# Strassen-type products for the feed-forward up projections of a two-layer hybrid decoder trunk

## The chip, the cores and the metric

The kernel runs on one NeuronCore of one Trainium2 chip. The metric is the device time of one execution in microseconds (us), the median of several runs. Engines are named as the profile names them: PE is TensorE's matmul, PEld its weight load, DVE is VectorE, ACT is ScalarE, POOL is GpSimd, SP is SyncE, whose queue issues the DMAs.

## The reference

Two layers on x of 1024 tokens x 1024 channels in float32. Layer 0 mixes tokens with forgetting attention, layer 1 with a Conformer convolution module; each mixer is followed by a gated feed-forward block with a causal convolution of width 3.

```python
for i in range(2):
    h = rms_norm(x, mixer_gain)
    x = x + (fox_attention if i == 0 else conformer_conv)(h, ...)
    h = rms_norm(x, ffn_gain)
    x = x + conv_ffn(h, w_up, w_dw, b_dw, w_down)

def conv_ffn(h, w_up, w_dw, b_dw, w_down):      # w_up (1024, 5632), w_down (2816, 1024)
    u = causal_dwconv(h @ w_up, w_dw) + b_dw    # width 3
    gate, val = split(u, 2)
    return (silu(gate) * val) @ w_down

def conformer_conv(h, ...):                     # inner width 1024
    a, g = split(h @ w_pw1 + b_pw1, 2)
    u = causal_dwconv(a * sigmoid(g), w_dw) + b_dw   # width 31
    return silu(rms_norm(u, ln_g)) @ w_pw2 + b_pw2
```

## The kernel before, in words

All matrix products run in a split form: each float32 operand is written as a high part (rounded to the matmul's type by an ACT cast) and a low part (the remainder, a subtraction on POOL or DVE), and `mm3` makes three matmuls of them: high x high, high x low, low x high. A weight tile comes by `weight`: DMA into `raw`, then `split` into `whi` (ACT, L132) and `wlo` (POOL, L133). The matmuls themselves all stand on L138 to L140, so they are told apart by the tile that they write: `up` and `pw` (`pw1`) for the projections up, `dn` for the projections down, `wops` for the attention's output projection, `pj` for its inputs, `nps` for the transposes in a norm.

The order of instructions on each engine is made when the kernel is built: a scheduler takes the work in the order in which the program text emits it (earlier is more urgent) and places an instruction when its inputs and its buffer are there. Emission order is set by Python generators that are stepped against each other.

Tokens are held as two halves of 512. The normed, transposed activations of a half are `hthi` and `htlo`, 8 tiles of 128 channels by 512 tokens. For a feed-forward half, `ffn` runs over 22 channel steps `f`. `up_tile(f)` makes the gate tile and the value tile, each 8 x 3 = 24 matmuls of 128x128 weights on 512 tokens into one PSUM bank; ACT scales the bank into `acc` (L214), DVE adds the two earlier taps (L219), for the second half also the taps that reach into the first half's last tokens (`edge`, L224), ACT applies Silu to the gate (L228), DVE multiplies (L233) and the product is split into `ahi`, `alo` (L236, L237), which stay in SBUF. Every four steps, `down_half` multiplies these by the matching rows of w_down into one of two `dn` banks, 12 matmuls for a block of 128 tokens by 512 channels, and DVE adds the bank to x (L193; L176 in `down`).

x stays in SBUF as 8 tiles of 128 tokens. After the last addition to a block of tokens, `norm_block` norms and transposes it: ACT squares and sums (L110), POOL makes the reciprocal root (L102, L103), DVE scales (L112), PE transposes (L119), ACT and DVE write the high and low parts (L123, L127).

The convolution module of a half is `conv`: `glu` makes two banks of `pw1` (48 matmuls) and `u`; `taps_of` sums 31 taps, 21 of them on DVE (L718, into PSUM) and 10 on ACT and POOL (L722, L723); after all eight channel tiles come the norm (`sqa`, L732) and the projection `pw2`, whose bias POOL adds to x beforehand (L668). While a half is in `conv`, its x is parked in DRAM (`xd`).

The two layers' feed-forward and convolution work is laid side by side by the emission order: layer 0 half 0's feed-forward first, then layer 0 half 1's together with the convolution of half 0 (2 feed-forward steps to 3 convolution steps), then layer 1 half 0's feed-forward together with the convolution of half 1, then layer 1 half 1's. At each change, the first items of the next are alternated with the last of the one before.

Of the kernel before, what the change touches and what calls it, by code (L numbers as in the profile page):

```python
# [43 lines left out]
RAW_BUFS = 2  # L44
WHI_BUFS = 5
WLO_BUFS = 5
ACC_BUFS = 4
ACT_BUFS = 6
# [4 lines left out]
FFN_ITEMS = 88  # L53
LEAD = 4
LAG = 6
TAIL = 2
RATIO = (2, 3)
GAP = 3


class Trunk:
    def __init__(self, ctx, tc):
# [4 lines left out]
        self.hp = ctx.enter_context(tc.tile_pool(name="ht", bufs=1, reuse_waits="tile"))  # L67
# [22 lines left out]

    def ht_half(self, h):
        return tuple(
            self.hp.tile([P, KT, 512], F32R, tag=f"{m}{h}", name=self.n(f"{m}{h}")) for m in ("hthi", "htlo")
        )
# [10 lines left out]
    def norm_block(self, scr, psum, tag, xt, gain, ht, tb, stag="scr"):  # L105
# [7 lines left out]
        hi, lo = ht[tb // 4]  # L113
        c = slice((tb % 4) * P, (tb % 4 + 1) * P)
        for q in range(KT // 4):
            ps = psum.tile([P, 4, P], F32, tag=tag, name=self.n("nps"))
            for j in range(4):
                k = 4 * q + j
                nc.tensor.transpose(ps[:, j, :], hn[:, k * P : (k + 1) * P], self.ident)  # L119
            for j in range(4):  # L120
                k = 4 * q + j
                g = gain[:, k : k + 1]
                nc.scalar.activation(hi[:, k, c], ps[:, j, :], AF.Copy, scale=g)  # L123
            for j in range(4):
                k = 4 * q + j
                g = gain[:, k : k + 1]
                nc.vector.scalar_tensor_tensor(  # L127
                    lo[:, k, c], ps[:, j, :], g, f32(hi[:, k, c]), op0=ALU.mult, op1=ALU.subtract
                )

# [4 lines left out]
    def mm3(self, out, lh, ll, rh, rl, start, stop):  # L135

        nc = self.nc
        nc.tensor.matmul(out, lh, rh, start=start, stop=False)  # L138
        nc.tensor.matmul(out, lh, rl, start=False, stop=False)  # L139
        nc.tensor.matmul(out, ll, rh, start=False, stop=stop)  # L140
# [14 lines left out]
    def weight(self, src, shape):  # L155

        raw = self.wp.tile(shape, F32, tag="raw", name=self.n("raw"), bufs=RAW_BUFS)
        self.nc.sync.dma_start(raw, src)
        hi = self.wp.tile(shape, F32R, tag="whi", name=self.n("whi"), bufs=WHI_BUFS)
        lo = self.wp.tile(shape, F32R, tag="wlo", name=self.n("wlo"), bufs=WLO_BUFS)  # L160
        self.split(hi, lo, raw)
        return hi, lo

    def down(self, xs, h, lhs, rows, after):

        nc = self.nc
        ws = [self.weight(r, [P, D]) for r in rows]
        for b in range(4):
            tb = 4 * h + b
            c = slice(b * P, (b + 1) * P)  # L170
            for nh in range(2):
                m = slice(nh * 512, (nh + 1) * 512)
                ps = self.pdn.tile([P, 512], F32, tag="dn", name=self.n("dn"))
                for j, (hi, lo) in enumerate(lhs):
                    self.mm3(ps, hi[:, c], lo[:, c], ws[j][0][:, m], ws[j][1][:, m], j == 0, j == len(lhs) - 1)
                nc.vector.tensor_tensor(xs[tb][:, m], xs[tb][:, m], ps, op=ALU.add)  # L176
            if after is not None:
                after(tb)
            yield

    def down_half(self, xs, h, lhs, rows, nh):
# [3 lines left out]
        ws = [self.weight(r[:, m].rearrange("(k p) n -> p k n", p=P), [P, 2, 512]) for r in rows]  # L185
        for b in range(4):
            tb = 4 * h + b
            c = slice(b * P, (b + 1) * P)
            ps = self.pdn.tile([P, 512], F32, tag="dn", name=self.n("dn"))
            for j, (hi, lo) in enumerate(lhs):  # L190
                wh, wl = (w[:, j % 2, :] for w in ws[j // 2])
                self.mm3(ps, hi[:, c], lo[:, c], wh, wl, j == 0, j == len(lhs) - 1)
# [3 lines left out]
    def ffn(self, l, xs, h, ht, w_up, w_down, tab, edge, after):  # L196
# [7 lines left out]
        def up_tile(f):  # L204
            accs = []
            for s in range(2):
# [23 lines left out]
                if s == 0:  # L230
                    yield
# [695 lines left out]
```

## Time and profile before

| what | value |
|---|---|
| median of 3 runs | 2415.11 us (2413.39 to 2418.46) |
| profiled execution, its own time | 2417.31 us |
| span of that execution, first to last instruction | 2415.6 us |
| PE, PEld busy | 98%, 84% |
| DVE, ACT, POOL busy | 60%, 50%, 53% |
| mean granted PE clock | 0.994 |
| DMA | 235.40 MB, mean 97 GB/s |
| attention and its output projection end | about 667 us into the span |

Busy time of PE is a matmul's modelled duration, and neighbours overlap, so 98% does not say by itself that PE could not go faster. Idle time that is listed in front of a group of instructions is put down to what ended it. Times in the views below are us from the start of the span unless they end in ns.

### The profile page before, as it was taken

To read this page: it belongs to the slowest core of one execution; us is meant where nothing else is said; L and a number is where in the kernel's file an instruction comes from. 1 tells how busy PE (TensorE), PEld (TensorE's weight loads), DVE (VectorE), ACT (ScalarE), POOL (GpSimd) and SP (SyncE) were. 2 spreads that over 40 slices of the span, in tenths; PEclk is the share of its full clock that TensorE was granted. 3 is DMA by queue.
4 is the path that set the end of the run, shared out by engine and by line. 5 is a ranking of instruction groups with operands and counts; after the bars stand their busy time and mean duration, and the time that the engine had idled before them with its cause. 6 is when DMAs were issued, how large, how long until landed. Compare 5 with 4: busy or idle time off the path is not lost.

```text
span 2415.6 us, 32653 instructions
## 1 busy us (share of the span) xinstructions
PE 2361.5 (98%) x11822; PEld 2028.0 (84%) x11822; DVE 1457.3 (60%) x2773; ACT 1200.6 (50%) x2241; POOL 1274.4 (53%) x886
## 2 busy tenths in 40 slices
PE   7899999989999999999999999999999999999999
PEld 6899999988888888888878878788888887888887
DVE  5577777776353333376868775747767656644444
ACT  6466666665253333355555552545655543333332
POOL 2355544543054444466777763648778644444442
PEclk9999999999999999999999999999999999999999
DMA  4222222154033333243233333333233233333332
GB/s 127 64 79 80 80 76 76 58 178 141 5 118 96 96 97 96 88 133 94 88 104 88 97 109 118 114 96 105 88 99 102 88 130 114 105 105 96 96 96 79
DMA packets 308978, 235.40 MB, mean 97 GB/s; under 512 B 12328, under 2 KB 272208, under 8 KB 308816
## 3 DMA queue, kind: packets, MB, share of 16 engines
q1 hardware_dynamic: 308816, 233.32, 31.6%
q8 instruction: 93, 1.52, 0.3%
q14 instruction: 69, 0.57, 0.1%
HBM read 209.61 MB, written 15.27 MB: 93 GB/s over the span
## 4 chain that ended last, share of the span: by engine, by line
PE 81%; DVE 9%; ACT 3%; POOL 2%; issue 2%; DMA 2%; SPq 0%; POOLq 0%; ACTq 0%; DVEq 0%
PE up L139 11%; PE up L140 11%; PE up L138 11%; PE dn L138 6%; PE dn L140 6%; PE dn L139 6%; PE pj L138 4%; PE pj L139 4%; PE pj L140 4%; PE pT L482 2%; DVE cacc L718 2%; PE s L453 2%; PE pw L139 1%; PE pw L138 1%; DVE acc L219 1%
## 5 line engine op out<-in xcount | busy, mean ns | idle before, releaser
L133 POOL TENSOR_TENSOR wlo<-raw,whi 128x1024 fp32r<-128x1024 f32 (+1 forms) x340 | 804.1, 2372 | 650.7 <-ACT whi L132 633.5
L139 PE MATMUL up<-htlo,whi 128*128 128x512 f32 x1408 | 548.9, 390 | 0.0
L140 PE MATMUL up<-hthi,wlo 128*128 128x512 f32 x1408 | 548.5, 390 | 0.0
L138 PE MATMUL up<-hthi,whi 128*128 128x512 f32 x1408 | 548.0, 390 | 0.0
L132 ACT CAST whi<-raw 128x1024 fp32r<-128x1024 f32 (+2 forms) x344 | 353.8, 1030 | 376.7 <-PE dn L140 157.8
L219 DVE SCALAR_TENSOR_TENSOR acc<-up,ffntab,acc 128x511 f32<-128x511 f32 x352 | 262.3, 745 | 351.0 <-ACT edge L217 200.0
L138 PEld LDWEIGHTS up<-hthi,whi 128*128 128x128 f32 x1408 | 264.3, 188 | 54.7
L139 PEld LDWEIGHTS up<-htlo,whi 128*128 128x128 f32 x1408 | 264.4, 188 | 54.5
L140 PEld LDWEIGHTS up<-hthi,wlo 128*128 128x128 f32 x1408 | 264.4, 188 | 54.2
L138 PE MATMUL dn<-whi,ahi 128*128 128x512 f32 x704 | 277.0, 393 | 7.6 <-DVE x L193 7.6
L140 PE MATMUL dn<-whi,alo 128*128 128x512 f32 x704 | 275.4, 391 | 1.0 <-DVE alo L237 1.0
L139 PE MATMUL dn<-wlo,ahi 128*128 128x512 f32 x704 | 275.3, 391 | 0.0
L718 DVE SCALAR_TENSOR_TENSOR cacc<-u,ctaps,cacc 128x512 f32<-128x512 f32 x320 | 240.8, 753 | 7.4
L193 DVE TENSOR_TENSOR x<-x,dn 128x512 f32<-128x512 f32 x176 | 119.8, 681 | 167.7 <-PE dn L140 167.6
L723 POOL TENSOR_TENSOR pacc<-pacc,prod 128x512 f32<-128x512 f32 x144 | 194.3, 1349 | 33.3 <-ACT prod L722 27.7
L138 PE MATMUL pj<-whi,hthi 128*128 128x384 f32 (+1 forms) x512 | 180.9, 354 | 6.3 <-ACT sqr L380 3.5
L139 PE MATMUL pj<-wlo,hthi 128*128 128x384 f32 (+1 forms) x512 | 178.8, 349 | 0.5 <-DVE wlo L133 0.5
L140 PE MATMUL pj<-whi,htlo 128*128 128x384 f32 (+1 forms) x512 | 179.1, 350 | 0.0
L102 POOL TENSOR_SCALAR ss<-ss 128x4 f32<-128x4 f32 (+1 forms) x96 | 20.7, 215 | 275.9 <-ACT hn L110 124.5
L138 PEld LDWEIGHTS dn<-whi,ahi 128*128 128x128 f32 x704 | 133.0, 189 | 37.7 <-DVE x L193 9.8
L236 ACT CAST ahi<-acc 128x512 fp32r<-128x512 f32 x88 | 54.6, 620 | 219.8 <-DVE acc L233 219.8
L140 PEld LDWEIGHTS dn<-whi,alo 128*128 128x128 f32 x704 | 132.8, 189 | 29.2 <-DVE alo L237 1.4
(166 smaller groups left out, 4334.0 us busy)
## 6 DMA issues: line engine op xcount, KB each, us to landing
raw<-in_ffn_w_up_dram SPq DMA_DIRECT2D x176, 512.0 KB
raw<-in_ffn_w_down_dram SPq DMA_DIRECT2D x88, 512.0 KB
raw<-in_conv_w_pw_dram SPq DMA_DIRECT2D x48, 512.0 KB
raw<-in_fox_w_in_dram SPq DMA_DIRECT2D x64, 192.0 KB
nct<-ncd SPq DMA_DIRECT2D x16, 512.0 KB
xin<-in_x_dram SPq DMA_DIRECT2D x8, 512.0 KB
kd<-kd SPq DMA_DIRECT2D x64, 64.0 KB
kl<-kl SPq DMA_DIRECT2D x64, 64.0 KB
```

The source lines that it names most:

```text
L132: self.nc.scalar.copy(hi, raw)
L133: (self.nc.vector if vector else self.nc.gpsimd).tensor_tensor(lo, raw, f32(hi), op=ALU.subtract)
L138: nc.tensor.matmul(out, lh, rh, start=start, stop=False)
L139: nc.tensor.matmul(out, lh, rl, start=False, stop=False)
L140: nc.tensor.matmul(out, ll, rh, start=False, stop=stop)
L193: nc.vector.tensor_tensor(xs[tb][:, m], xs[tb][:, m], ps, op=ALU.add)
L219: nc.vector.scalar_tensor_tensor(acc[:, j:], ps[:, : 512 - j], tap[2 - j], acc[:, j:], op0=ALU.mult, op1=ALU.add)
L236: nc.scalar.copy(hi, b)
L453: nc.tensor.matmul(po, lh, ds[c]["kd"][:, h, :], start=True, stop=False)
L482: nc.tensor.transpose(tr[:, b * P : (b + 1) * P], prow[i][:, kt * P : (kt + 1) * P], self.ident)
L718: nc.vector.scalar_tensor_tensor(acc, win(j), tap(j), acc, op0=ALU.mult, op1=ALU.add)
L723: nc.gpsimd.tensor_tensor(pacc, pacc, t, op=ALU.add)
```

## The change

The up projections are no longer done for one half of the tokens at a time. `up` handles, for each step f, the 2x2 block product of weights and activations in the seven-product form of Strassen's scheme (Winograd's variant). The weight blocks are a11, a12 (the first and second 512 input channels of the gate tile) and a21, a22 (the same of the value tile); the activation blocks are b11, b21 (first token half, first and second 512 channels) and b12, b22 (second token half). Each product is 4 x 3 = 12 matmuls into a bank. The sums of weight blocks (s1 to s4) are made on POOL for each f, the sums of activation blocks (t1 to t4, high and low parts of each) once per layer in `combine`, from a second half that `to_whole` leaves unsplit in float32. The intermediate sums of products (p1, u2, u3) are added in PSUM or SBUF by DVE, and the taps follow as before for all four results (gate and value, two halves).

The gated channels are written to DRAM (`actd`, 22 tensors of 128x1024) and read back and split by a separate down phase, `down_acts`, which holds four banks for four token blocks and runs over all 22 steps, for each half of the output channels. x goes to DRAM after each norm and comes back (`fetch_x`) when a projection is added to it; its SBUF is shared with t2, t3, t4 and the convolution's `ys`.

The emission order is now: up of layer 0 for both halves; down of layer 0 half 0; down of half 1 with the convolution of half 0 (1 down step to 2 convolution steps); the rest of that convolution with the convolution of half 1 (1 to 2); up of layer 1; down of layer 1, half 0 and half 1. pw1 weights come in pieces of 128x512 instead of 128x1024, and the buffers are: raw 8, split 9 (each of 2 KB a partition; before 2 and 5 of 4 KB), six `up` banks (before four and two `dn`), `acc` 5, `half` 4, `sum` 4.

```diff
+    def combine(self, ht0, b12, b22):
...
+        for kt in range(4):
...
+            v.tensor_tensor(t["t1"], x12, f32(b11h[:, kt, :]), op=ALU.subtract)
+            v.tensor_tensor(t["t1"], t["t1"], f32(b11l[:, kt, :]), op=ALU.subtract)
+            v.tensor_tensor(t["t2"], x22, t["t1"], op=ALU.subtract)
+            put("t2", kt, t["t2"])           # put: ACT cast to high, DVE subtraction to low
+            v.tensor_tensor(t["t3"], x22, x12, op=ALU.subtract)
+            put("t3", kt, t["t3"])
+            put("t1", kt, t["t1"])
+            put("b22", kt, x22)
+            v.tensor_tensor(t["t4"], f32(b21h[:, kt, :]), t["t2"], op=ALU.subtract)
+            v.tensor_tensor(t["t4"], t["t4"], f32(b21l[:, kt, :]), op=ALU.add)
+            put("t4", kt, t["t4"])

+    def up(self, l, fac, w_up, tab, actd):
...
+        for f in range(NF):
+            (a11, a12), (a21, a22) = (
+                [self.load(wu[:, 4 * j : 4 * j + 4, ft * P : (ft + 1) * P], shape) for j in range(2)] for ft in fts
+            )
...
+            for o, x, y, op in (
+                (s1, a21, a22, ALU.add), (s2, s1, a11, ALU.subtract),
+                (s3, a11, a21, ALU.subtract), (s4, a12, s2, ALU.subtract),
+            ):
+                nc.gpsimd.tensor_tensor(o, x, y, op=op)
+            def product(ps, left, right, first):
+                lh, ll = self.halves(left, shape)
+                rh, rl = fac[right]
+                for k in range(4):
+                    self.mm3(
+                        ps, lh[:, k, :], ll[:, k, :], rh[:, k, :], rl[:, k, :], first and k == 0, k == 3, not first
+                    )
...
+            def gated(h):
+                a, b = accs.pop((0, h)), accs.pop((1, h))
+                nc.vector.tensor_tensor(b, a, b, op=ALU.mult)
+                nc.sync.dma_start(actd[f][:, h * 512 : (h + 1) * 512], b)
+            x, y = bank("c11"), bank("c21")
+            product(x, a11, "b11", True)
+            p1 = half("p1")
+            nc.scalar.copy(p1, x)
+            product(y, s2, "t2", True)
+            u2 = half("u2")
+            nc.vector.tensor_tensor(u2, y, p1, op=ALU.add)
+            product(x, a12, "b21", False)
+            e0 = taps(0, 0, x, None)
+            product(y, s3, "t3", False)
+            u3 = half("u3")
+            nc.vector.tensor_tensor(u3, y, p1, op=ALU.add)
+            z, w = bank("c12"), bank("c22")
+            product(z, s1, "t1", True)
+            nc.vector.tensor_tensor(w, z, u3, op=ALU.add)
+            product(y, a22, "t4", False)
+            nc.vector.tensor_tensor(y, y, p1, op=ALU.add)
+            e1 = taps(1, 0, y, None)
+            gated(0)
+            product(z, s4, "b22", False)
+            taps(1, 1, w, e1)
+            nc.vector.tensor_tensor(z, z, u2, op=ALU.add)
+            taps(0, 1, z, e0)
+            gated(1)

+    def down(self, xs, h, nh, lhs, rows, after=None):
+        m = slice(nh * 512, (nh + 1) * 512)
+        pss = [self.pup.tile([P, 512], F32, tag="up", name=self.n("dn")) for _ in range(4)]
+        for j, (get, r) in enumerate(zip(lhs, rows)):
+            hi, lo = get()                   # down_acts: load from actd, low part on DVE
+            wh, wl = self.weight(r[:, m], [P, 512])
+            for b in range(4):
+                c = slice(b * P, (b + 1) * P)
+                self.mm3(pss[b], hi[:, c], lo[:, c], wh, wl, j == 0, j == len(lhs) - 1)
+            yield
+        for b in range(4):
+            tb = 4 * h + b
+            nc.vector.tensor_tensor(xs[tb][:, m], xs[tb][:, m], pss[b], op=ALU.add)
+            if after is not None:
+                after(tb)
+        yield

+    ffn_up(0, keep)
...
+        run(ffn_down(0, 0, xds[0], conv_norm))
+        c0, c1 = conv(0), conv(1)
+        run(until(ffn_down(0, 1, xds[0], conv_norm), c0, *DOWN_CONV))   # DOWN_CONV = (1, 2)
+        run(alternate(c0, c1, 1, 2))
+    ffn_up(1, keep1)
+    for h in range(2):
+        run(ffn_down(1, h, xds[2], lambda tb: nc.sync.dma_start(a["out"][0, tb * P : (tb + 1) * P, :], xs[tb])))
```

`until` now runs until its first generator ends (before: its second). `conv_norm` norms a block for the convolution, lets POOL add the pw2 bias to x and stores x; `taps` is the former tap code for one of the four results.

More of the change, by code (lines that the diff above doesn't have):

```diff
@@ L253, in ffn @@
-        last = groups[-1]
-        yield from self.down(xs, h, [acts[f] for f in last], [wd[f * P : (f + 1) * P, :] for f in last], after)
+                accs[s, h] = acc
+                return mine
+            def gated(h):
[4 more added lines that the diff above has]
+            product(x, a11, "b11", True)
```

340 lines of the change are left out of this document (161 added, 179 removed).

## The prediction

> **What bounds the kernel now.** I read the page's first and fourth parts, then stretches of the span, then costs by line.
>
> ```profile
> span 2415.6 us, 32653 instructions
> ...
> PE 2361.5 (98%) x11822; PEld 2028.0 (84%) x11822; DVE 1457.3 (60%) x2773; ACT 1200.6 (50%) x2241; POOL 1274.4 (53%) x886
> ...
> PE 81%; DVE 9%; ACT 3%; POOL 2%; issue 2%; DMA 2%; SPq 0%; POOLq 0%; ACTq 0%; DVEq 0%
> ```
>
> TensorE (PE) is busy for 98% of the span and carries 81% of the chain that ended last. Busy time can hide gaps, so here are five stretches after the attention. The columns are start:end, length, then busy time and (count) of PE, its weight loads, VectorE (DVE), ScalarE (ACT) and GpSimd (POOL), then granted clock, DMA share, GB/s.
>
> ```profile
> 700.00:980.00 280.00, 280.00 (x1237) 231.94 (x1236) 98.44 (x139) 102.60 (x159) 124.10 (x52) 1.00 0.33 98
> 1040.00:1440.00 400.00, 393.35 (x1737) 324.45 (x1736) 302.37 (x453) 217.02 (x315) 286.83 (x164) 0.99 0.33 100
> 1440.00:1560.00 120.00, 116.12 (x529) 94.03 (x528) 74.23 (x128) 54.55 (x106) 58.45 (x37) 1.00 0.34 110
> 1560.00:1960.00 400.00, 399.09 (x1777) 330.38 (x1776) 275.43 (x385) 224.62 (x347) 285.99 (x161) 1.00 0.34 103
> 1960.00:2416.00 456.00, 447.77 (x1985) 369.21 (x1984) 225.56 (x353) 154.41 (x216) 191.15 (x87) 1.00 0.31 98
> ```
>
> In the pure feed-forward stretch 700 to 980 PE never pauses: 1237 matmuls in 280 us, 0.2264 us from one 512-column matmul to the next, which is my price of a matmul (its row says 390 ns, but neighbours overlap). Where a convolution half is mixed with feed-forward work (1040 to 1440, 1560 to 1960), POOL is busy 72% and DVE 76 and 69% of the time, and PE loses only 6.7 and 0.9 us (3.9 between). That mixing is the cover that this change gives up in part.
>
> **What is removed.** Before, one gate/value pair of a 128-channel step, both token halves, takes 4 tiles x 24 = 96 matmuls. After, `up` makes 7 products of 4 x 3 = 12: 84. With 22 pairs and 2 layers, 2 x 22 x 12 = 528 matmuls go: 528 x 0.2264 = **119.5 us less**, as long as PE stays the bound. Down, pw1 and pw2 keep their counts.
>
> **One step of `up`, engine by engine.** PE: 84 x 0.2264 = 19.0 us.
>
> ```profile
> L133 POOL TENSOR_TENSOR wo<-raw,wo x6: 1293/1302/2735, 552.1 to 573.3; 128x512 fp32r<-128x512 f32 x6
> L193 DVE TENSOR_TENSOR x<-x,dn 128x512 f32<-128x512 f32 x176 | 119.8, 681 | 167.7 <-PE dn L140 167.6
> L219 DVE SCALAR_TENSOR_TENSOR acc<-up,ffntab,acc 128x511 f32<-128x511 f32 x176 | 131.8, 749 | 348.7 <-ACT edge L217 200.0 <-ACT acc L214 148.5
> L224 DVE SCALAR_TENSOR_TENSOR acc<-edge,ffntab,acc 128x1 f32<-128x1 f32 x88 | 84.2, 957 | 0.0
> L224 DVE SCALAR_TENSOR_TENSOR acc<-edge,ffntab,acc 128x2 f32<-128x2 f32 x88 | 44.5, 506 | 0.0
> L233 DVE TENSOR_TENSOR acc<-acc,acc 128x512 f32<-128x512 f32 x88 | 70.0, 796 | 1.4
> L214 ACT ACTIVATE acc<-up,ffntab 128x512 f32<-128x512 f32 x176 | 135.9, 772 | 27.8 <-PE up L140 27.8
> L236 ACT CAST ahi<-acc 128x512 fp32r<-128x512 f32 x88 | 54.6, 620 | 219.8 <-DVE acc L233 219.8
> L228 ACT ACTIVATE acc<-acc 128x512 f32<-128x512 f32 x88 | 55.6, 632 | 127.1 <-DVE acc L224 88.6 <-DVE acc L219 38.3
> ```
>
> POOL makes 4 weight sums and 7 low parts of 128x512, 1.30 us each (median of the first row): 14.3 us. DVE: five combinations with a PSUM input (0.68), eight tap passes (0.75), edges 2 x (0.96 + 0.51), two gate products (0.80): 3.4 + 6.0 + 2.9 + 1.6 = 13.9 us. ACT: seven casts and one copy at 0.62, four scaled copies at 0.77, two Silu at 0.63, small edge copies: about 9.6 us. All lie beside PE's 19.0, at 75, 73 and 50%: the loads of the stretch 1560 to 1960, where PE lost 0.9 us in 400. So the step costs PE's time.
>
> What is new is four short hand-offs: p1 copied before the third product rewrites bank x, u2 and u3 added before y is rewritten, w before z is. Each reader has one product's length, 12 x 0.2264 = 2.7 us. The down projection's two banks have exactly this slack now.
>
> ```profile
> PE dn L138 <- DVE x L193: 7.6, 5, 2.2
> PE dn L138 <- DVE x L176: 1.7, 2, 1.4
> ```
>
> PE waited 9.3 us for them, and evictions in loaded stretches number, by my estimate, some 100 to 120 of the 176 on the first row's line and its sister's. At 0.08 us, 4 x 44 hand-offs cost **14 us**; bounds 0 and, if each step were late by one 1 us edge operation, 44.
>
> **The start of each up phase.**
>
> ```profile
> 819.44 0.69 DVE L237 TENSOR_TENSOR alo<-acc,ahi 128x512 fp32r<-128x512 f32 x1 [0.69 <-ACT ahi L236]
> L110 ACT ACTIVATE hn<-x 128x1024 f32<-128x1024 f32 x24 | 25.8, 1073 | 64.5 <-DVE x L176 32.1 <-DVE x L627 21.9 <-issue 10.5
> L123 ACT ACTIVATE hthi<-nps,gtab 128x128 fp32r<-128x128 f32 x192 | 53.6, 383 | 44.5 <-PE nps L119 27.8 <-PE wops L139 16.6
> L103 POOL TENSOR_TENSOR ss<-ss,mhalf 128x1 f32<-128x1 f32 x32 | 17.9, 558 | 2.6
> 667.27 0.39 PE L138 MATMUL up<-hthi,whi 128*128 128x512 f32 x1
> 669.60 0.65 PE L119 MATMUL nps<-ident,hn 128*128 128x128 f32 x4 [1.71 <-DVE htlo L127]
> ```
>
> `combine` needs the second half's normed tokens complete: 4 x 11 DVE operations. At 0.69 us (first row) that is 30 us, and the second product needs its 36th, at 25 us. Before that PE can do 4 whole products (first and third of two steps) and three quarters of three more: 48 + 27 matmuls, 17 us. Ahead of `combine` stands a norm.
>
> Layer 0: last block's add 0.68, square 1.07, root 0.56, scaling some 0.75, two rounds of four transposes at 0.65, copies: 5 us. Layer 1: all four blocks are normed after the last pw2 pass, ACT spending 1.07 + 4 x 0.38 and small change on each, some 13 us. Idle: 5 + 25 - 17 = 13 and 13 + 25 - 17 = 21. But `combine` reads two SBUF operands in every operation, and this is what such an operation does beside POOL:
>
> ```profile
> 686.86 2.60 POOL L133 TENSOR_TENSOR wlo<-raw,whi 128x1024 fp32r<-128x1024 f32 x1 [2.64 <-ACT whi L132]
> 687.89 2.12 DVE L237 TENSOR_TENSOR alo<-acc,ahi 128x512 fp32r<-128x512 f32 x1 [0.69 <-ACT ahi L236]
> L237 DVE TENSOR_TENSOR alo<-acc,ahi 128x512 fp32r<-128x512 f32 x18 | 13.9, 772 | 12.4 <-ACT ahi L236 12.4
> L237 DVE TENSOR_TENSOR alo<-acc,ahi 128x512 fp32r<-128x512 f32 x20 | 23.0, 1150 | 6.8 <-ACT ahi L236 6.5
> L133 POOL TENSOR_TENSOR wlo<-raw,whi 128x1024 fp32r<-128x1024 f32 x312 | 752.3, 2418 | 645.2 <-ACT whi L132 628.0 <-PE up L139 4.7 <-DMA raw<-in_ffn_w_down_dram 4.3
> ```
>
> The DVE subtraction (0.69 us alone) began 1.0 us after POOL's and ended 0.55 after it; its mean rises from 772 to 1150 ns from the light stretch (700 to 980) to the loaded one (1560 to 1960). The Trainium skill, SBUF — State Buffer, "Who interferes with whom", says that a DVE operation with two SBUF inputs and a GpSimd operation that reads SBUF shut each other out, the later one waiting for the whole of the other. By that rule none of the 44 would overlap a POOL operation, and the two rows of 687 agree for DVE's side; for POOL's they show 2.60 against a mean of 2.42. In layer 0 POOL has about 17 weight operations to make just then: between 0 and 17 x 1.30 = 22 us more, I take 11. In layer 1 the weights can be ready. **24 + 20 = 44 us**; bounds 25 and 65. Now up follows the last output projection at once (667.27) with one gap of 1.71.
>
> **The down phases.** A step is 12 matmuls, 2.72 us, with two casts (1.24), one POOL (1.30) and one DVE (0.69) low part; even shut out against each other 2.0 us. DMA: 512 KB per 2.72 us = 193 GB/s.
>
> ```profile
> 530.00:535.00 5.00, 2.67 (x23) 2.38 (x22) 3.88 (x12) 4.67 (x12) 2.87 (x5) 1.00 1.03 411
> L158 SPq DMA_DIRECT2D raw<-in_ffn_w_up_dram x176: 367/368/2345, 585.6 to 2356.1; - x176
> ```
>
> 411 GB/s has run here, and SP issues a load in 0.37 us, two per step. In `up`, six issues take 2.2 of 19 us; the store waits on SP for the gate product with the next weights queued behind it, but eight raw buffers hold two steps. The activations go out once and come back twice; up weights are read once instead of twice. x goes out and back three times instead of once, one pass (60 us) ahead of its use. What hides all this is PE's 2.72 a step; were a step 0.1 longer, 176 of them would cost 18 us. I take **0**, with 7 us for the seams where banks change hands (three, 1 to 3 us each; bounds 0 and 15).
>
> **The convolution.** Half 0 now runs under the down of half 1 only (two conv steps per down step), half 1 under the rest of half 0's pw2. From the end of the first down phase to half 1's last tap, POOL has:
>
> ```profile
> L723 POOL TENSOR_TENSOR pacc<-pacc,prod 128x512 f32<-128x512 f32 x144 | 194.3, 1349 | 33.3 <-ACT prod L722 27.7
> L732 POOL TENSOR_TENSOR sqa<-sqa,sq 128x512 f32<-128x512 f32 x14 | 18.6, 1327 | 11.4 <-ACT sq L731 11.4
> L668 POOL TENSOR_TENSOR x<-x,b 128x512 f32<-128x512 f32 x16 | 21.2, 1346 | 7.7 <-DVE hn L112 7.7
> ```
>
> Low parts 44 (down) + 64 (pw1) + 16 (pw2 of half 0) = 124 x 1.30 = 161; tap sums 144 x 1.35 = 194; squares 14 x 1.33 = 19; bias 16 halves x 1.35 = 22; twelve norms' roots 7: **403 us**. DVE's 52 low parts beside them may hold POOL up by 0 to 52 x 0.69 = 36; I take half: 421.
>
> ```profile
> L718 DVE SCALAR_TENSOR_TENSOR cacc<-u,ctaps,cacc 128x512 f32<-128x512 f32 x320 | 240.8, 753 | 7.4
> ```
>
> DVE's own share (336 tap passes x 0.75 = 253, the rest some 120) stays below. PE has 528 + 768 + 192 matmuls = 337 us and 12 blocks of transposes, 12: 349. So PE idles 72, and 10 more while half 1's norm runs from last tap to first pw2 product: **82 us**; bounds 45 (POOL's rows at their cheapest, below) and 115.
>
> ```profile
> 2410.79 0.39 PE L140 MATMUL dn<-whi,alo 128*128 128x512 f32 x1
> ```
>
> The end: four 512 KB stores after the last add, 5.1 us at 411 GB/s and the add, against 4.8 us now: **3 us**. What goes: the present pauses, 6.7 + 3.9 + 0.9 + 3.4 (8.2 less the tail) + 1.7 = **17 us**.
>
> **Sum.** -119.5 + 14 + 44 + 7 + 82 + 3 - 17 = +13.5, on a span of 2415.6: **2429 us**. That execution took 2417.3 and the median is 2415.1, 2.2 lower; the 1.7 around the span and this cancel, so 2429 stands for the median too. 0.2% (5 us) is about what this kernel's measurement can tell.
>
> **Rivals.**
> A, faster: POOL's instructions in the conv stretch cost less. Half of a 128x1024 low part is 1.21 and the tap sum could run at 1.30: 150 + 187 + 19 + 22 + 7 = 385 and no blocking, 36 less: 2393. For it: POOL is serial and DVE's blocking is seen only where POOL happened to run. Against: the 512-wide row says 1.30. It decides (faster) below a stretch of 402.
> B, the products' chain bounds: DVE's edge operations, locked behind POOL, delay u2 by 1 us a step beyond the 14 us: 44 more, 2473. For it: 957 ns on average for one column. Against: the loaded stretch's 0.9 us.
> C, POOL loses every microsecond that DVE's two-SBUF operations take, and they every one of POOL's: conv stretch 403 + 36, which is 18 more than I took, and 11 more in layer 0's start: 2458. For it: 1150 against 772. Against: POOL's 1.35 mean beside such operations is hardly longer than 1.30. It is the case that the Trainium skill's rule, quoted above (SBUF — State Buffer), would have.
> D, no change: gaps of 120 us in all, 2410 to 2420.
>
> **Chances.** Forecast, 2420 to 2448: 0.36. A and its neighbourhood under 2410: 0.35. C 0.10, B 0.09, D 0.10. So faster 0.35, same 0.10, slower 0.55. The range leaves out the lowest and highest tenth: 2385 to 2475; the slower cases alone lie within 2420 to 2480.
>
> **What would show it.** Right: 1848 up matmuls per layer at 0.226 us and PE over 97% in the up phases; PE idle 13 to 35 us at each start with `combine` on DVE; in the conv stretch POOL over 90% busy and PE near 80%. Wrong: PE under 95% within `up` waiting for DVE or ACT (B); a conv stretch of 400 or less, or POOL clearly below 90% there (A, or a bound I missed); down steps over 2.8 us, with DMA late.

## The result, and the profile after

The changed kernel takes **2558.7 us** (median of 4 runs, 2557.3 to 2561.4) against 2416.2 in the same comparison: ratio 1.059 [1.0573, 1.061], 142 us slower. The forecast was 2429, range 2385 to 2475: the sign was right, the size was far outside the range. This is the page of the changed kernel; its rows answer to the first fence of the prediction, and the rows with 40 digits are the span in 40 slices of 64 us.

```profile
span 2556.4 us, 34333 instructions
...
PE 2292.2 (90%) x11294; PEld 1944.0 (76%) x11294; DVE 1659.9 (65%) x2945; ACT 1272.2 (50%) x2621; POOL 1527.2 (60%) x1322
...
PE   7999999989689999999989958941889999999999
...
PEclk9999999999889999999999978975889999999999
...
PE 80%; DVE 9%; POOL 5%; issue 3%; ACT 2%; DMA 1%; SPq 0%; POOLq 0%; DVEq 0%; ACTq 0%
```

The 528 matmuls are gone (11822 to 11294), and PE's busy time fell from 2361.5 to 2292.2 us. But PE is now empty for 264 us of its span, where it was empty for 54. The digits show where: a dip at slices 11 and 12, holes at slices 24 and 27 to 28, another dip at 29 and 30. The clock row sinks at the same places. The windows give the same by stage (columns as in the prediction: length, busy time and count of PE, PEld, DVE, ACT, POOL, then clock, DMA share, GB/s).

```profile
650.00:700.00 50.00, 28.74 (x121) 21.96 (x121) 32.60 (x34) 16.09 (x34) 27.14 (x22) 0.79 0.31 97
700.00:750.00 50.00, 36.91 (x125) 25.77 (x124) 39.10 (x51) 20.19 (x35) 28.59 (x20) 0.77 0.16 48
...
850.00:900.00 50.00, 47.65 (x208) 38.38 (x207) 30.66 (x48) 21.01 (x40) 34.62 (x27) 1.00 0.26 79
...
1500.00:1550.00 50.00, 16.16 (x69) 13.31 (x67) 18.30 (x28) 19.89 (x34) 40.04 (x34) 0.65 0.30 96
...
1700.00:1773.00 73.00, 0.00 (x0) 0.00 (x0) 64.51 (x96) 32.70 (x49) 50.68 (x40) 0.50 0.03 13
1277.00:1773.00 496.00, 367.52 (x1615) 300.32 (x1613) 378.82 (x560) 277.50 (x524) 411.10 (x321) 0.87 0.36 114
...
2400.00:2450.00 50.00, 50.00 (x222) 41.41 (x221) 27.94 (x23) 21.06 (x38) 23.89 (x18) 1.00 0.72 235
```

Four things are to be read. The start of the first up phase (650 to 750) loses 34 of 100 us. The steady up phase has 208 matmuls in 50 us instead of the 222 of an unbroken row. The convolution stretch, from the end of the first down phase to the last tap sum of half 1, takes 496 us with PE busy for 368. The down phase is what was forecast: PE without a gap at 235 GB/s. The chain of PE's waits names the places:

```profile
PE ssps L828 <- POOL sqa L815: 113.7, 2, 83.8
PE c L167 <- DVE u L323: 34.5, 44, 0.8
PE c L168 <- DVE blo L232: 21.3, 9, 12.6
PE c L167 <- ACT bhi L231: 18.1, 9, 4.2
...
PE c L167 <- DVE u L318: 4.5, 2, 2.2
```

L828 is the convolution norm's first matmul (both halves: 114 us, one of them 84). `u` at L323 is u3 in `up`, once in each of the 44 steps; u2, at L318, made PE wait twice in all. `blo` and `bhi` are the parts of the combinations at the two up starts.

### The profile page after: what moved, and what is told of

Read it like the earlier page. It is cut to its first block, busy times and chain, and to the rows that moved or that the text cites. A ratio compares the mean times of both kernels' runs of the same rounds, so it can differ in the third digit from the quotient of the medians.

```text
span 2556.4 us, 34333 instructions
## 1 busy us (share of the span) xinstructions
PE 2292.2 (90%) x11294; PEld 1944.0 (76%) x11294; DVE 1659.9 (65%) x2945; ACT 1272.2 (50%) x2621; POOL 1527.2 (60%) x1322
## 4 chain that ended last, share of the span: by engine, by line
PE 80%; DVE 9%; POOL 5%; issue 3%; ACT 2%; DMA 1%; SPq 0%; POOLq 0%; DVEq 0%; ACTq 0%
PE c L167 11%; PE c L168 11%; PE c L169 11%; PE dn L168 6%; PE dn L167 6%; PE dn L169 6%; PE pj L167 3%; PE pj L168 3%; PE pj L169 3%; POOL pacc L806 3%; PE pT L574 2%; DVE cacc L801 2%; PE pw L168 2%; PE pw L167 2%; PE pw L169 2%
## 5 line engine op out<-in xcount | busy, mean ns | idle before, releaser
L162 POOL TENSOR_TENSOR wlo<-raw,whi 128x512 fp32r<-128x512 f32 (+1 forms) x432 | 589.8, 1369 | 311.9 <-ACT whi L161 284.6
L161 ACT CAST whi<-raw 128x512 fp32r<-128x512 f32 (+2 forms) x612 | 367.8, 630 | 462.2 <-PE dn L168 199.7
L167 PE MATMUL c<-bhi,whi 128*128 128x512 f32 x880 | 352.9, 402 | 57.4 <-DVE u L323 34.5
L162 POOL TENSOR_TENSOR wlo<-sum,whi 128x512 fp32r<-128x512 f32 x176 | 249.3, 1417 | 233.6 <-ACT whi L161 233.6
L294 DVE SCALAR_TENSOR_TENSOR acc<-c,ffntab,acc 128x511 f32<-128x511 f32 (+1 forms) x352 | 255.9, 746 | 192.5 <-ACT edge L292 134.1
L168 PE MATMUL c<-blo,whi 128*128 128x512 f32 x880 | 349.1, 397 | 21.3 <-DVE blo L232 21.3
L169 PE MATMUL c<-bhi,wlo 128*128 128x512 f32 x880 | 346.0, 393 | 0.0
L168 PE MATMUL dn<-wlo,whi 128*128 128x512 f32 x704 | 276.9, 393 | 2.3 <-POOL wlo L162 2.3
L169 PE MATMUL dn<-whi,wlo 128*128 128x512 f32 x704 | 275.3, 392 | 0.0
L167 PE MATMUL dn<-whi,whi 128*128 128x512 f32 x704 | 269.7, 391 | 1.6 <-ACT whi L161 1.6
```

Of the source, the lines that this page charges most:

```text
L161: self.nc.scalar.copy(hi, raw)
L162: (self.nc.vector if vector else self.nc.gpsimd).tensor_tensor(lo, raw, f32(hi), op=ALU.subtract)
L167: nc.tensor.matmul(out, lh, rh, start=start, stop=False, skip_group_check=more)
L168: nc.tensor.matmul(out, lh, rl, start=False, stop=False, skip_group_check=more)
L169: nc.tensor.matmul(out, ll, rh, start=False, stop=stop, skip_group_check=more)
L294: nc.vector.scalar_tensor_tensor(acc[:, j:], ps[:, : 512 - j], tap[2 - j], acc[:, j:], op0=ALU.mult, op1=ALU.add)
```

## The experiments

Four questions stood: what the step's wait at u3 costs, what the combinations cost, what the order of the stages costs without Strassen, and what makes the convolution stretch long. Times are medians; the kernel before took 2416 to 2418 in every comparison.

**1. A bank of its own for the sixth product.** In the changed kernel the fifth product of a step stands ahead of the third on PE, so that the fourth (s3·t3) and the sixth (a22·t4) are neighbours, on one bank, with u3's read between them:

```profile
911.98 0.39 PE L169 MATMUL c<-bhi,wlo 128*128 128x512 f32 x1
913.15 0.50 PE L167 MATMUL c<-bhi,whi 128*128 128x512 f32 x1 [0.79 <-DVE u L323]
```

```
-            product(y, a22, "t4", False)
-            nc.vector.tensor_tensor(y, y, p1, op=ALU.add)
-            e1 = taps(1, 0, y, None)
+            v = bank("c21b")
+            product(v, a22, "t4", True)
+            nc.vector.tensor_tensor(v, v, u3, op=ALU.add)
+            e1 = taps(1, 0, v, None)
```

> The sixth product of an up step (a22 times t4) gets a PSUM bank of its own, and u3 is added to it afterwards, so the products s3*t3 and a22*t4 no longer stand one behind the other on one bank with VectorE's read of u3 between them. Nothing is left out. Theory 1 (the hand-off to u3 is the up step's loss): in the changed kernel's trace that place has 1.17 us between two matmuls instead of 0.23, in each of 44 steps, 44 x 0.94 = 41 us; expected 2558.7 - 41 = 2518 us, between 2510 and 2528, with TensorE at 49 of 50 us in the up stage. Rival (the step is paced by GpSimd's sums and low parts or by the next hand-off, and the wait moves to the next place): within 10 us of 2558.7.

Measured: 2510.9 us (ratio to before 1.0383 [1.0368, 1.0399]), **47.8 us gained**. The same 50 us of the up phase, in this kernel:

```profile
850.00:900.00 50.00, 50.00 (x222) 41.42 (x221) 33.26 (x53) 23.34 (x43) 36.98 (x29) 1.00 0.25 80
```

Theory 1 holds, and the wait did not move elsewhere: 222 matmuls again. That a step's other engines (DVE 33, POOL 37 of 50 us) do not pace it was forecast, and is so.

**2. Plain products in the same order of stages.** Eight products a step, no combinations, everything else as changed:

```
+            def tile_of(s, h, e):
+                ps = bank("c")
+                product(ps, ("a11", "a21")[s], ("b11", "b12")[h], True)
+                product(ps, ("a12", "a22")[s], ("b21", "b22")[h], False)
+                return taps(s, h, ps, e)
```

> The Strassen products are undone, the rest of the change is kept: eight plain products a step over both halves at once, both halves' norms split as the first one's was, no combinations, gated channels through DRAM, separate down phase, the convolution beside the second down phase. Theory 2 (the new order of the stages costs more than the products save): 528 more matmuls x 0.2264 = +119.5, the u3 hand-offs gone -41, the combinations gone from the two starts -40 to -60; about 2558.7 + 119.5 - 41 - 50 = 2587 us, between 2560 and 2610, that is 145 to 195 us above the kernel before, with the convolution stretch as long as in the changed kernel. Rival (the Strassen step's own waits are the loss and the order is cheap): 2420 to 2470 us.

Measured: 2558.1 us (1.0583 [1.0564, 1.0602]), the same as the changed kernel. The line of busy times of its page and its rows (its convolution stretch lies 8 us earlier, 1269 to 1765):

```profile
PE 2376.8 (93%) x11822; PEld 2039.2 (80%) x11822; DVE 1385.8 (54%) x2669; ACT 1165.3 (46%) x2437; POOL 1108.2 (43%) x1014
...
650.00:700.00 50.00, 48.22 (x217) 39.49 (x217) 19.05 (x48) 23.78 (x58) 18.26 (x19) 0.97 0.52 159
700.00:750.00 50.00, 50.00 (x222) 41.40 (x221) 18.73 (x35) 14.79 (x27) 10.46 (x9) 1.00 0.24 75
...
1269.00:1765.00 496.00, 367.74 (x1616) 300.56 (x1614) 380.18 (x560) 277.09 (x524) 410.92 (x321) 0.87 0.37 118
```

This splits the 142 us. The order of stages (both halves at once, separate down, convolution with little beside it) costs about 142 us by itself, with the same convolution stretch, 496 us with PE busy for 368, so 128 empty. Over the whole span (2557.7 us) PE is empty for 181 us, 127 more than before, and its busy time is 15 us longer for the same 11822 matmuls, at a mean granted clock of 0.964 against 0.994. On top of this order the Strassen products gain nothing: what they save is given back within the up phase. The expectation was 29 us too high, 21 of them because I had taken both give-backs too small (41 where experiment 1 had 47.8, 50 where the next one has 64).

**3. Without the combinations.** t1 to t4 are not made, and other factors take their places:

```
-        made = {"b22": new(False), "t2": new(True), "t3": new(True), "t1": new(False), "t4": new(True)}
+        made["t1"], made["t2"], made["t3"], made["t4"] = made["b22"], (b21h, b21l), (b11h, b11l), made["b22"]
```

> Leaves out the Strassen combinations t1 to t4 at both up starts (40 of 44 VectorE instructions; the products take other ready factors, so the output is another); all else stays. Theory 4 (the combinations, made at 1.7 us an instruction because VectorE and GpSimd hold each other up, are most of the starts' loss): the two starts lose about 38 us each in the changed kernel, and 25 of it goes in each; 2558.7 - 50 = 2509 us, between 2498 and 2522. Rival (the starts wait for the last norms and the first weights in any case): 0 to 20 us gained, 2539 to 2559 us.

Measured: 2494.9 us (1.0313 [1.0295, 1.033]), **63.8 us gained**: about 37 of them in layer 0's start (the norm matmul behind half 1's last tap comes at 1740.6 us instead of 1777.2) and 26 in layer 1's. Not all of it is the combinations themselves: the factors that stand in for t2 and t3 belong to the first half, and in layer 1's start they let 48 matmuls run ahead of the last blocks' norm instead of 12, which is 8 us. So the up phase gives back 47.8 + 63.8 = 111.6 of the 119.5 us of saved matmuls, which is the tie of the run before within 8 us.

The two starts differ. First VectorE and GpSimd in layer 0's start, then VectorE in layer 1's start, where GpSimd had nothing to do between 1840 and 1861, and GpSimd at a time when VectorE stood still; all are rows of the changed kernel:

```profile
687.48 1.76 DVE L232 TENSOR_TENSOR blo<-b,bhi 128x512 fp32r<-128x512 f32 x1
689.16 1.75 DVE L246 TENSOR_TENSOR t<-hthi,t 128x512 f32<-128x512 f32 x1
```

```profile
686.98 1.71 POOL L268 TENSOR_TENSOR sum<-raw,raw 128x512 f32<-128x512 f32 x1
688.66 1.70 POOL L162 TENSOR_TENSOR wlo<-sum,whi 128x512 fp32r<-128x512 f32 x1
```

```profile
1849.98 0.68 DVE L246 TENSOR_TENSOR t<-hthi,t 128x512 f32<-128x512 f32 x1
1850.58 0.68 DVE L238 TENSOR_TENSOR t<-b,hthi 128x512 f32<-128x512 f32 x1
```

```profile
1802.45 1.29 POOL L268 TENSOR_TENSOR sum<-sum,raw 128x512 f32<-128x512 f32 x1
```

Alone, a VectorE instruction starts every 0.60 us. Beside each other both engines step at 1.68 us, in turn, and the added time stands inside their durations (1.75 where VectorE alone has 0.68, 1.70 where GpSimd alone has 1.29). The Trainium skill, SBUF — State Buffer, "Who interferes with whom", says that VectorE with two SBUF inputs and a GpSimd instruction that reads SBUF keep each other off; here the trace agrees, on both engines. It is mostly a matter of layer 0's start. Windows from the first to the last of the 44 instructions, layer 0's start, then layer 1's:

```profile
675.90:728.10 52.20, 22.56 (x51) 12.77 (x51) 51.96 (x51) 22.03 (x40) 39.06 (x23) 0.60 0.18 52
1844.30:1878.10 33.80, 18.26 (x43) 10.41 (x42) 33.63 (x51) 16.05 (x30) 7.74 (x5) 0.60 0.01 3
```

They take 52 us with GpSimd busy for 39, and 34 us with GpSimd busy for 8: the difference of some 18 us is, by my estimate, the two engines' standing in each other's way. But both starts are long without that, because PE has little to do meanwhile: 51 and 43 matmuls, at 0.2264 us each 11.5 and 9.7 us of work.

**4. Combinations on TensorE.** On top of experiment 1, t1 to t4 are summed in PSUM by matmuls with plus and minus the identity, and VectorE only makes 16 low parts out of PSUM:

```
+                ms = [(sg, m[:, kt, :]) for b, sg in ts for m in made[b]]
+                for i, (sg, m) in enumerate(ms):
+                    nc.tensor.matmul(ps, self.eye[sg], m, start=i == 0, stop=i == len(ms) - 1)
```

> Built on the kernel with the sixth product's own bank (2510.9 us). The four combinations are made by TensorE as sums of products with plus and minus the identity matrix in PSUM (22 matmuls for each of 4 channel blocks, 88 a start), and VectorE makes 16 low parts out of PSUM instead of 44 instructions between SBUF tiles. Theory 4 (the combinations cost the starts 32 us each because VectorE's instructions with two SBUF sources and GpSimd's hold each other up): TensorE works 88 x 0.2264 = 20 us a start on them, VectorE is out of the way, each start 10 to 18 us shorter: 2475 to 2491 us. Rival (the starts wait for the high and low parts in any case, or the extra matmuls cost what they save): 2503 to 2520 us.

Measured: 2496.4 us (1.0331 [1.0316, 1.0347]), 14.5 us less than experiment 1's 2510.9, somewhat under the expectation, and all of it in layer 0's start: the norm matmul behind half 1's last tap comes 17 us earlier than in experiment 1 (1737.9 against 1755.1), and nothing more is gained behind it, where layer 1's start lies. PE in 650 to 750 is busy for 91.5 us, 20 of them with combinations (88 x 0.2264), where experiment 1 had 66.4:

```profile
650.00:700.00 50.00, 41.51 (x181) 33.33 (x180) 22.64 (x51) 23.52 (x61) 24.70 (x24) 0.90 0.32 95
700.00:750.00 50.00, 50.00 (x222) 41.40 (x221) 27.36 (x43) 22.81 (x40) 32.52 (x26) 1.00 0.21 64
```

**5. Taps out of the convolution.** First without ScalarE's and GpSimd's nine products and sums a channel tile:

```
-                    nc.scalar.activation(t, win(done), AF.Copy, scale=tap(done))
-                    nc.gpsimd.tensor_tensor(pacc, pacc, t, op=ALU.add)
```

> Leaves out the nine tap products and sums per channel tile that ScalarE and GpSimd make in the convolution (16 tiles x 9 sums), so that the output is another; VectorE's 21 taps stay. Theory 3 (GpSimd bounds the convolution stretch, 1277 to 1773 us): 144 sums x 1.34 = 193 us of its work go, TensorE's 349 us become the bound with norm and tail beside them; 2558.7 less 100 to 140 = 2420 to 2460 us, and TensorE's empty time between 1500 and 1550 and between 1700 and 1770 is gone. Rival (the stretch is long because of the order of work and of the PSUM banks that the norm's transposes and VectorE's taps share): less than 40 us gained, above 2520 us.

Measured: 2503.4 us (1.0357 [1.034, 1.0373]), 55 us gained: between the two theories. GpSimd lost 193 us of work, but VectorE's own taps took its place in the tail. A group of 36 passes from the timeline (start, length):

```profile
1674.87 23.79 DVE L801 SCALAR_TENSOR_TENSOR cacc<-u,ctaps,cacc 128x512 f32<-128x512 f32 x36
```

A pass starts every 0.66 us (23.79 for 36), so 21 of them take 13.9. In the changed kernel's tail GpSimd's tile is as long (nine sums 12.03, a square 1.27, a wait of 1.5):

```profile
1731.11 12.03 POOL L806 TENSOR_TENSOR pacc<-pacc,prod 128x512 f32<-128x512 f32 x9
1744.78 1.27 POOL L815 TENSOR_TENSOR sqa<-sqa,sq 128x512 f32<-128x512 f32 x1 [1.64 <-DVE cacc L801]
1746.10 12.03 POOL L806 TENSOR_TENSOR pacc<-pacc,prod 128x512 f32<-128x512 f32 x9
```

So in the second run 29 of 31 taps were left out, on both engines:

```
-                else:
-                    nc.vector.scalar_tensor_tensor(acc, win(j), tap(j), acc, op0=ALU.mult, op1=ALU.add)
-                while done < (n_pool - 1) * (i + 1) // nv:
...
```

> The changed kernel (2558.7 us) with 29 of the convolution's 31 taps left out (VectorE's 20 and GpSimd's 9), so that the output is another. Theory 3b (in the tail VectorE's 21 taps at 0.66 us and GpSimd's sums take the same 14 to 15 us a channel tile, so taking away one alone gained 55): without both, the tail of half 1 (84 us) and that of half 0 (30 us) go: 2558.7 - 115 = 2444 us, between 2425 and 2465. Rival (norm chain, order and banks hold TensorE back, whatever the taps take): 2495 us and more.

Measured: 2440.5 us (1.0098 [1.0083, 1.0113]), **118 us gained**, as expected. The stretch ends at 1656 instead of 1773: it shrinks from 496 to 379 us, and PE is busy for 363 of them:

```profile
1277.00:1656.00 379.00, 362.75 (x1624) 298.59 (x1622) 157.37 (x240) 185.62 (x382) 224.12 (x179) 0.98 0.47 150
```

**6. Another order of the same work.** The second down phase goes one to one with half 0's convolution, half 1's first projection ahead of half 0's last taps, half 0's second projection later; in the second run only the ratio `1, 2` of the changed kernel becomes `1, 4`:

```
-DOWN_CONV = (1, 2)
+DOWN_CONV = (1, 1)
...
-        run(alternate(c0, c1, 1, 2))
+        run(itertools.islice(c0, 26))
+        run(itertools.islice(c1, 2))
+        run(itertools.islice(c0, 8))
+        run(alternate(c0, c1, 1, 3))
```

> The changed kernel (2558.7 us) with another order of the same work around the convolution, nothing left out: the second down phase is interleaved one to one with half 0's convolution, so that it ends first and half 0's own first pointwise products fill TensorE while half 1 is normed; half 1's first channel tile is projected before half 0's last is tapped; then one step of half 0's second pointwise product to three of half 1. Theory 3d (the two tails are empty because the work that could fill TensorE has been used up ahead of the taps): of half 0's tail (34 us empty in 1500 to 1550) 20 to 30 come back, of half 1's (84 us) the 43 us of half 0's second pointwise product at most; 2494 us, between 2480 and 2520. Rival (the taps' rate on VectorE and GpSimd sets the end of the stretch, in any order): 2540 us and more.

> The changed kernel (2558.7 us) with one number changed: in the stretch of half 1 one step of half 0's rest goes to four of half 1 instead of two, so that half 0's second pointwise product (16 steps x 2.72 = 43 us of TensorE) and the norm behind it come later. Theory 3d: half 1's taps start earlier and part of the 43 us lies beside its tail: 15 to 43 us gained, 2516 to 2544 us. Rival (the taps' rate sets the end): within 8 us of 2558.7.

Measured: 2554.4 (1.056 [1.0545, 1.0576]) and 2561.0 us (1.0592 [1.0577, 1.0608]). My theory fell: PE's work can be moved about, but the end of half 1's taps stays within 3 us of where it was. The norm matmul behind the last tap of half 1, first in the changed kernel, then in these two (first and last start of 16):

```profile
L828 PE MATMUL ssps<-ones,sqa x16: 352/352/372, 1541.0 to 1777.2; 128*128 128x1 f32 x16
```

```profile
L828 PE MATMUL ssps<-ones,sqa x16: 344/352/374, 1582.9 to 1774.4; 128*128 128x1 f32 x16
```

```profile
L828 PE MATMUL ssps<-ones,sqa x16: 352/352/372, 1540.8 to 1780.0; 128*128 128x1 f32 x16
```

**7. GpSimd's share of the taps, down and up:**

```
-N_POOL = 10
+N_POOL = 7        (in the second run: 12)
```

> The changed kernel (2558.7 us) with the convolution's taps divided otherwise, nothing left out: 7 instead of 10 of the 31 taps go to ScalarE and GpSimd, 24 instead of 21 to VectorE. 16 tiles x 3 = 48 sums of 1.34 us leave GpSimd (-64), 48 taps of 0.66 us come to VectorE (+32). Theory 5 (GpSimd's rate sets the end of the convolution stretch): 25 to 60 us gained, 2500 to 2534 us. Theory 6 (VectorE's rate sets it as much, both take some 15 us a channel tile): the tail's tiles become 24 x 0.66 + 1.4 = 17 us instead of 14.9, five tiles +11, and the earlier part gains a little; 2550 to 2580 us.

> The same number the other way: 12 taps to ScalarE and GpSimd, 19 to VectorE: 32 sums x 1.34 = +43 us on GpSimd, 32 x 0.66 = -21 us on VectorE. Theory 5: 20 to 43 us longer, 2579 to 2602 us. Theory 6: GpSimd's tile of the tail becomes 11 x 1.34 + 1.27 = 16 us instead of 13.3, just above VectorE's 13.9: 5 to 20 us longer, 2564 to 2579 us.

Measured: 2542.0 us with 7 (1.0522 [1.0506, 1.0538], 16.7 gained), 2605.8 with 12 (1.0786 [1.0768, 1.0804], 47.1 lost). The stretch with 7 (it ends at 1757), then with 12 (at 1821):

```profile
1277.00:1757.00 480.00, 365.07 (x1612) 298.34 (x1610) 405.00 (x608) 244.38 (x476) 348.51 (x273) 0.88 0.37 118
```

```profile
1277.00:1821.00 544.00, 375.34 (x1611) 302.26 (x1609) 365.72 (x528) 301.84 (x556) 448.89 (x352) 0.84 0.33 104
```

Going up, the loss is slightly more than all the added GpSimd work (43 us): from 10 on GpSimd sets the rate. Going down, a quarter of the 64 us taken off GpSimd is gained, and VectorE is then the fuller one (405 against 349). VectorE's waits for GpSimd's tap sums say the same: 5.6 us in all with 7, 22.9 with 10, 56.4 with 12. Neither theory had both signs and sizes: GpSimd is the bound at 10, with VectorE close behind it.

**8. Banks for the norm's transposes.** In the changed kernel they share two PSUM banks with VectorE's tap sums; here the norms in the convolution (the line shown) and after it use the product banks:

```
-            T.norm_block(T.scr, pst, "t", xs[tb], T.to_split(gains[1], hc[tb // 4]), tb)
+            T.norm_block(T.scr, T.pup, "up", xs[tb], T.to_split(gains[1], hc[tb // 4]), tb)
```

> The changed kernel (2558.7 us) with the transposes of the norms in and after the convolution moved to the product banks, so that VectorE's tap sums no longer share two PSUM banks with them. Nothing is left out. Theory 3c (the shared banks hold VectorE's taps back for some 35 us, 1652 to 1692 us in the changed kernel): 20 to 40 us gained, 2519 to 2539 us. Rival (the taps' own length sets the tail): within 8 us of 2558.7.

Measured: 2539.4 us (1.051 [1.0494, 1.0526]), 19.3 gained: the banks did hold the taps back, just short of what was expected.

**9. Cover for half 1.** On top of experiment 1, layer 1's up products are plain and made half by half, so that the convolution of half 1 has them beside it:

```
+        run(until(c0, c1, 1, 2))
+        u0 = up1(0)
+        run(until(c1, u0, 1, 1))
+        run(u0)
+        run(up1(1))
```

> Built on the kernel with the sixth product's own bank (2510.9 us). Layer 0 keeps the Strassen products; layer 1's up projections are plain and made half by half, so that the convolution of half 1 runs beside the up products of layer 1's half 0, which need nothing of half 1. Theory 2 (the change's order leaves the convolution's second half with nothing for TensorE beside it): back come 264 matmuls x 0.2264 = +60; gone are TensorE's empty time while the last channel tiles are tapped (84 in one wait), the empty time at layer 1's up start (about 35) and part of the norm and second pointwise product's waits (10 to 20): 2511 + 60 - 84 - 35 - 15 = 2437 us, between 2405 and 2460. Rival (GpSimd and VectorE, not the missing cover, set the time: with taps and layer 1's weights together they are the bound): 2490 us and more.

Measured: 2504.9 us (1.0363 [1.0346, 1.038]), 6 us less than experiment 1 with 264 matmuls (60 us) more. PE's empty time fell from 231 (span 2510.2, busy 2278.8) to 171 us (2507.7, 2337.1), by 61 and not by the 134 that I had added up. The longest wait of half 1 is gone, but half 0's is not covered by this, and others stay (PE's waits in 1250 to 1550, 1550 to 1800 and 1800 to 2000; L868 is the norm's first matmul here):

```profile
PE ssps L868 <- POOL sqa L855: 31.1, 1, 31.1
...
PE nps L125 <- DVE htlo L139: 13.0, 5, 3.3
...
PE ssps L868 <- POOL sqa L855: 13.0, 1, 13.0
```

So cover is part of the answer (84 us became 13 in that wait), not the whole that theory 2 made of it.

**10. Do the mends add up?** All of 1, 4, 6 (its first order) and 8; then the same without the order of 6; then 9 with 4 and 8:

> All mends together: the sixth product's own bank (-48), combinations on TensorE (-14.5 beside it), norm transposes in the product banks (-19), and the order of the run before last (expected -65). If the gains add: 2558.7 - 48 - 14.5 - 19 - 65 = 2412 us, beside 2416 of the kernel before, between 2395 and 2440. Rival (the mends of the stretch overlap, the same empty time is counted twice): 2440 to 2485 us, still slower than before.

> The mends without the other order: the sixth product's own bank, the combinations on TensorE, the norms' transposes in the product banks; nothing is left out. If the last two are independent: 2496.4 - 19.3 = 2477 us, between 2468 and 2488, and the other order of the run with all mends (2489.9) was a loss beside them. Rival: the norm's banks gain only while the starts are long, 2489 to 2500 us.

> Strassen products in layer 0 alone, layer 1 plain by halves beside the convolution's half 1, with the sixth product's own bank, the combinations of layer 0 on TensorE and the norms' transposes in the product banks. The run without the last two took 2504.9; one start instead of two gets shorter (-7 to -10) and two of the three norms change banks (-10 to -19): 2480 us, between 2470 and 2490, still above the kernel before. Rival (in this version the norms' transposes, 13 and 26 us of waits, are on TensorE's path, and their banks free more): 2440 to 2465 us.

Measured: 2489.9 (1.0294 [1.0277, 1.0311]), 2478.7 (1.0257 [1.0242, 1.0273]) and 2476.0 us (1.0244 [1.0228, 1.0259]). Bank, combinations and transposes add (47.8 + 14.5 + 19.3 = 81.6 forecast, 80.0 found); the other order costs 11 beside them. No version that does the whole work passes the kernel before; the best is 58 us slower.

## Why the prediction was wrong

The error is 2558.7 - 2429 = 130 us. The forecast named the places where the change loses, and three of its terms were too small; they hold 121 of the error (67, 20 and 34), and 9 are left over between them.

- **The convolution, with seams, tail and old pauses: 82 + 7 + 3 - 17 = 75 forecast, 142 measured** (experiment 2, the order alone). The step that failed is "So PE idles 72": I divided the stretch by GpSimd's work. That work was right, 421 us forecast, 411 in the row. But GpSimd was busy for 83% of 496 us, not for all of a stretch of 421, and PE was empty for 128 us of the 496. GpSimd had to wait for the first projections, in the gap between the halves, and for VectorE, whose tile is as long as its own. Three windows of the changed kernel hold 55 of its 85 idle us (GpSimd is the fifth busy time), and its longest wait lasts until VectorE's 32 passes in a row (1692.5 to 1713.7) are done:

```profile
1300.00:1325.00 25.00, 23.36 (x99) 18.25 (x99) 11.10 (x23) 11.51 (x27) 9.68 (x7) 0.94 0.46 146
1550.00:1600.00 50.00, 48.69 (x217) 40.02 (x218) 26.29 (x58) 31.01 (x71) 25.60 (x21) 0.94 0.28 90
1700.00:1725.00 25.00, 0.00 (x0) 0.00 (x0) 24.75 (x38) 7.63 (x12) 9.50 (x8) 0.50 0.09 38
...
1714.98 1.27 POOL L815 TENSOR_TENSOR sqa<-sqa,sq 128x512 f32<-128x512 f32 x1 [19.24 <-ACT sq L814]
```

My own mark, "POOL clearly below 90% there (A, or a bound I missed)", is met: the bound missed was VectorE, which I had set aside with "stays below". Leaving the taps out brings back 118 of the 142 us; the other 24 were not taken apart.

- **The starts: 44 forecast for everything, 64 measured when the combinations were left out** (experiment 3; about 37 in layer 0, 26 in layer 1). The step that failed is the cover, "PE can do 4 whole products (first and third of two steps) and three quarters of three more": 17 us were taken off in each start, and little of that was there. In the order in which the instructions stand, one product, 12 matmuls or 2.7 us, runs ahead of the first that reads a combination (at 683.2 and 1849.0 us); the rest stands behind it. GpSimd was the smaller part. Beside it a combination takes 1.75 us instead of 0.69, which made layer 0's 44 take 52 us where layer 1's took 34; for these 18 us I had taken 11, and 22 in rival C. Layer 1's start was mostly free of GpSimd's work, as forecast (8 us of 34). (By its own working layer 1's term is 21, not the 20 of the sum.)
- **The hand-offs: 14 forecast, 47.8 measured** (experiment 1). "Each reader has one product's length" failed at one of the four: u3's reader had none, because the product between was placed elsewhere. The others cost little, as forecast (4.5 us in all for u2). The size is that of rival B's bound of 44, but the cause is not B's, VectorE late by an edge operation: with another bank and the same VectorE work the loss is gone.

The terms together: 142 + 64 + 47.8 - 119.5 = 134 against 142.5 measured. The right steps: -119.5 for the matmuls (0.2264 us each in experiment 1), a down step of 2.72 us with nothing lost, DMA hidden, a step of `up` that costs PE's time once the bank is free. Of the rivals, A and D fell. C's mechanism shows in layer 0's start, for nearly the price it gave there; it is neither the starts' main loss nor the convolution's.

In the kernel before, the same taps lie between 1113 and 1914 us beside feed-forward products, so what lies within 448 us in the changed kernel (1325 to 1773) had 800 us with products beside it:

```profile
L718 DVE SCALAR_TENSOR_TENSOR cacc<-u,ctaps,cacc x320: 741/756/757, 1113.3 to 1914.2; 128x512 f32<-128x512 f32 x160
```

## What to carry to other kernels

When a stage loses its cover, do not divide the work by its fullest engine: list the second-fullest too, and the times at which both must wait for the first input and for each other (here 411 us of work took 496). A hand-off's slack is read from the order in which the instructions are in fact issued, not from the order of the source; the same order decides what can cover a start. In the up phase one bank more was worth 40% of what the products save (47.8 of 119.5 us). And an algorithm that needs all its inputs before its second product pays for that at its start and at the end of whatever comes ahead of it.

## What the runs showed of the hardware

Two things beside the steps of 1.68 us above, which I had expected for one engine and not in full for both. After a long wait TensorE starts slowly: behind the 84 empty us (1693 to 1777, granted clock 0.50 in the row of 1700 to 1773), the first matmuls of 512 columns start 0.43 us apart, and 3.5 us after the first they are back at 0.23 to 0.24.

```profile
1784.61 0.80 PE L167 MATMUL dn<-whi,hthi 128*128 128x512 f32 x1 [2.67 <-ACT hthi L842]
...
1786.48 0.63 PE L167 MATMUL dn<-whi,hthi 128*128 128x512 f32 x1
1786.91 0.63 PE L168 MATMUL dn<-wlo,hthi 128*128 128x512 f32 x1
...
1788.07 0.40 PE L167 MATMUL dn<-whi,hthi 128*128 128x512 f32 x1
1788.31 0.40 PE L168 MATMUL dn<-wlo,hthi 128*128 128x512 f32 x1
```

The Trainium skill, TensorE: Matmul & The Clock Gate, "Part 1: The HAM clock gate", gives half the clock after idling and full clock after some 3.4 us of work; the trace agrees. At 8 matmuls and 0.2 us each it is small change beside this hole. The other: VectorE's tap passes, with one vector in SBUF and one in PSUM, were never held up by GpSimd (shortest, median and longest of the changed kernel's 320, in a stretch where GpSimd was 83% busy), so the standstill belongs to two SBUF sources:

```profile
L801 DVE SCALAR_TENSOR_TENSOR cacc<-u,ctaps,cacc x320: 739/752/758, 1324.6 to 1765.1; 128x512 f32<-128x512 f32 x160
```
